# Column groups for the products of even and odd chunks at levels 32 and 64 of a gated recurrence

## The chip, the cores and the metric

One NeuronCore of a Trainium2 chip runs the whole kernel. The metric is device microseconds of one execution, as the median of several. Engines are named as in the profile: PE is TensorE's matrix multiplication, PEld its weight loads, DVE is VectorE, ACT is ScalarE, POOL is GpSimd, SP is SyncE.

## The reference, cut to what matters

A decoder layer on 1024 tokens of width 1024 in float32: a dilated attention and an HGRN2 recurrence, both fed by one large projection, merged by gates, then an output product and a norm. The change touches the recurrence alone. It has 8 heads with keys and values of 128:

```python
f = lb + (1.0 - lb) * jax.nn.sigmoid(f_raw)
k = 1.0 - f
# S_t = diag(f_t) S_{t-1} + k_t i_t^T;  o_t = S_t^T q_t
a = jnp.einsum('bhtk,bhsk,bhtsk->bhts', qc, kc, decay)
o_intra = jnp.einsum('bhts,bhsv->bhtv', a, vc)
```

The kernel takes chunks of 128 tokens, eight for each head, and needs for each chunk the 128 x 128 matrix `a` of decayed products of keys (rows, s) and queries (columns, t), for s up to t.

## The kernel before, in words

The kernel runs a projection (with products of split operands, three matmuls for each: lines 239 to 241), attention with more of the projection filled in between its steps, one branch product, the recurrence with the rest of the projection filled in, and the last two products. The change is in the recurrence stage, from about 553 to 960 us of the profiled span.

TensorE's instructions keep the order in which the program writes them (`manual_schedule` for PE); for the other engines the framework picks the order ahead of time. `recurrence(h)` is a generator: after each piece it yields an amount, and `fill(us)` then writes that many steps of the projection (`m` tiles, lines 239 to 241). The projection's weights are prepared two steps ahead: ACT casts them to `w_hi` (L246), DVE subtracts to `w_lo` (L224). A product's result is copied by ACT (L327) or added by DVE (L274).

In a head the chunk matrix is built by levels `hl` = 1, 2, 4, ..., 64. At a level the 1024 tokens fall into pairs of blocks of `hl`; the keys of the first block of a pair (`kk`) are multiplied with the decayed queries of the second (`qq`), and then DVE multiplies the decay of the level into `kk` (L1117) and `qq` (L1119) in place. Levels 1 to 16 go through `small()`: 32 matmuls with 32 stationary columns each, whose outputs go to the four groups of 32 partitions in turn (L1085). Their results are masked into `dg` by DVE (L1097, L1098) and copied into the diagonal blocks of `amat` (`am`) at L1135.

Level 32 has 16 matmuls in a burst (L1104), 32 stationary and 32 moving columns each. The first half of a chunk goes to partitions 0 to 31, the second to 64 to 95. Two ACT copies of 32 rows x 256 elements (L1107) bring them to `am`, rows in place. Level 64 has 8 matmuls (L1113), 64 stationary and 64 moving columns each, all of them to partitions 0 to 63, and one ACT copy of 64 x 512 (L1115). The stationary operand is a slice of `kk`, the moving one a slice of `qq`, all in float32, which the trace records as two loads and two matmuls for each matmul of the program. The results lie in `pp`, one bank of PSUM with two buffers.

After level 64 the keys are transposed (L1141), states are formed (L1153, L1157, L1159), and L1168 multiplies `am` with the values, L1170 the decayed queries with the states; the norm follows on ACT (L1173), DVE (L1175, L1177) and POOL (L1176), and its transposes (L1182) end the head.

Of the kernel before, what the change touches and what calls it, by code (L numbers as in the profile page):

```python
# [10 lines left out]
F32 = mybir.dt.float32  # L11
# [8 lines left out]
P = 128  # L20
# [159 lines left out]
def hybrid_layer(ctx: ExitStack, tc: tile.TileContext, x, w_ada, b_ada, w_in, w_branch_a, w_branch_b, w_out,  # L180
                 rel_bias, final_g, smalls, consts, onehot, logc, out, tap=None):
    nc = tc.nc
# [801 lines left out]
    with ExitStack() as ba:  # L984
# [5 lines left out]
        for m in range(4):  # L990
            for th in range(2):
                o, z = (b2p.tile([P, 512], F32, name="oar", bufs=7) for _ in range(2))
# [36 lines left out]
    with ExitStack() as hg:  # L1029
        g1 = hg.enter_context(tc.tile_pool(name="hg1", bufs=1, **right))  # L1030
        g2 = hg.enter_context(tc.tile_pool(name="hg2", bufs=2, **right))
        pp = hg.enter_context(tc.tile_pool(name="ps_p", bufs=2, **again))
# [5 lines left out]
        am = g1.tile([P, 8, P], F32, name="amat")  # L1038
        nc.gpsimd.memset(am, 0.0)
        qb = g1.tile([P, 2, S], F32, name="qb")  # L1040
        kk = g1.tile([P, S], F32, name="kk")
        qq = qb[:, 1]
        its, fqs, zss = {}, {}, {}

        def load_f(h):
            stream.need(f"f{h}")
            stream.need(f"h{h}")
            while turned.get(("i", h)) != 2:
                stream.step()
            fq = fqs[h] = g2.tile([P, S], F32, name="tot")  # L1050
            nc.sync.dma_start(fq, fb_d[h])
            nc.sync.dma_start(qb[:, 0], qb_d[h])
            it = its[h] = g2.tile([P, 8, P], F32, name="it")
            nc.sync.dma_start(it, ib_d[h])

        def load_z(h):
            zss[h] = []
            for th in range(2):
                z = g2.tile([P, 512], F32, name="zs")
                nc.sync.dma_start(z, zb_d[h][:, half_of(th)])  # L1060
                zss[h].append(z)
# [4 lines left out]
        def mask(n):  # L1066
            return kc[:, K_M + 32 * n:K_M + 32 * n + 32].unsqueeze(1).to_broadcast([P, 8, 32])

        def c3(t):
            return t.rearrange("p (c t) -> p c t", c=8)  # L1070

        def recurrence(h):
# [7 lines left out]
            def small(n):  # L1080
                pl = pp.tile([P, 512], F32, name="pp")[:, :256 * n].rearrange("p (c n t) -> p c n t", c=8, n=n)
                for c in range(8):
                    for b in range(4):
                        o = c * P + b * 32
                        nc.tensor.matmul(pl[32 * b:32 * b + 32, c], kk[:, o:o + 32], qb[:, 2 - n:2, o:o + 32],  # L1085
                                         start=True, stop=True)
                return pl

            n, hl = S // 2, 1
            while hl < P:  # L1090
                q4 = qq.rearrange("p (n two t) -> p n two t", two=2, t=hl)
                k4 = kk.rearrange("p (n two t) -> p n two t", two=2, t=hl)
                t3 = fq[:, :2 * n].rearrange("p (n two) -> p n two", two=2)
                if hl <= 16:
                    pl = small(2 if hl == 1 else 1)
                    if hl == 1:
                        nc.vector.tensor_tensor(d3, pl[:, :, 0], mask(0), ALU.mult)  # L1097
                    nc.vector.copy_predicated(d3, mask(1 + LEVELS.index(hl)).bitcast(I32), pl[:, :, 1 if hl == 1 else 0])  # L1098
                elif hl == 32:
                    pl = pp.tile([P, 512], F32, name="pp")[:, :256]  # L1100
                    for c in range(8):
                        for b in range(2):
                            o = c * P + 64 * b
                            nc.tensor.matmul(pl[64 * b:64 * b + 32, c * 32:c * 32 + 32], kk[:, o:o + 32],  # L1104
                                             qq[:, o + 32:o + 64], start=True, stop=True)
                    for b in range(2):
                        nc.scalar.copy(am[64 * b:64 * b + 32, :, 64 * b + 32:64 * b + 64],  # L1107
                                       c3(pl[64 * b:64 * b + 32]))
                else:
                    pl = pp.tile([P, 512], F32, name="pp")  # L1110
                    for c in range(8):
                        o = c * P
                        nc.tensor.matmul(pl[0:64, c * 64:c * 64 + 64], kk[:, o:o + 64], qq[:, o + 64:o + P],  # L1113
                                         start=True, stop=True)
                    nc.scalar.copy(am[0:64, :, 64:P], c3(pl[0:64]))  # L1115
                k_end = t3[:, :, 1:2].to_broadcast([P, n, hl])
                nc.vector.tensor_tensor(k4[:, :, 0, :], k4[:, :, 0, :], k_end, ALU.mult)  # L1117
                q_end = t3[:, :, 0:1].to_broadcast([P, n, hl])
                nc.vector.tensor_tensor(q4[:, :, 1, :], q4[:, :, 1, :], q_end, ALU.mult)  # L1119
                if fq is tot:  # L1120
                    tn = g1.tile([P, S // 2], F32, name="totn")
                    other = tot, tn
                else:
                    tn = other[0] if fq is other[1] else other[1]
                nc.vector.tensor_tensor(tn[:, :n], t3[:, :, 0], t3[:, :, 1], ALU.mult)
                fq = tn
                n //= 2
                hl *= 2
                yield 2.6
                if hl == 8:  # L1130
                    load_z(h)
                if hl == 32 and h + 1 < NHB:
                    load_f(h + 1)
# [14 lines left out]
            for g in range(2):  # L1148
                pu = pou.tile([P, 4, P], F32, name="pou")
                for cc in range(4):  # L1150
                    c = 4 * g + cc
                    if c < 7:
                        nc.tensor.matmul(pu[:, cc], kt[:, c], iv[:, c], start=True, stop=True)  # L1153
                for cc in range(4):
                    c = 4 * g + cc
# [7 lines left out]
            for g in range(2):  # L1163
                yield 1.9
                po = pou.tile([P, 4, P], F32, name="pou")
                for cc in range(4):
                    c = 4 * g + cc
# [30 lines left out]
        for h in range(NHB):  # L1198
            for us in recurrence(h):
                fill(us)  # L1200
# [250 lines left out]
```

## Time and profile before

| | |
|---|---|
| median of 3 runs | 1149.69 us (1147.69 to 1149.91) |
| the profiled execution's own time | 1151.74 us |
| its span, first to last instruction | 1149.9 us |
| mean granted clock of TensorE | 0.995 |
| PE busy | 97% of the span |
| DVE busy | 70% |
| ACT busy | 45% |

The span is the time between the first and the last instruction of the profiled execution; the rest of its own time lies around it. A busy share is the union of an engine's instructions. Matmuls are pipelined, so the duration of one is a latency, and what a burst of them costs is read from its first start to its last end. A line such as L1104 is a line of the kernel's file; a source line's matmul and its weight load are listed apart as PE and PEld.

### The profile page before, as it was taken

How to read it: one execution, taken by the hardware profiler on the slowest of the kernel's cores; microseconds unless marked ns; L12 is line 12 of the kernel's file. 1: busy time of each engine (PE TensorE's matmuls, PEld its weight loads, DVE VectorE, ACT ScalarE, POOL GpSimd, SP SyncE). 2: the span in 40 equal slices, each digit the busy share in tenths (PEclk: the TensorE clock that was granted, in tenths of full speed). 3: DMA queues.
4: the chain of work that ended last, by engine and by line, in shares of the span. 5: the costliest groups of instructions: out<-in, count | busy, mean ns of one | idle time of the engine just before them, and what ended most of it. 6: DMA issues, size and time to landing. Idle time of an engine off the chain costs nothing.

```text
span 1149.9 us, 21616 instructions
## 1 busy us (share of the span) xinstructions
PE 1113.1 (97%) x8266; PEld 908.7 (79%) x8266; DVE 809.0 (70%) x1607; ACT 517.8 (45%) x1059; POOL 117.7 (10%) x195
## 2 busy tenths in 40 slices
PE   5899999999999999999999999999999999999997
PEld 2677788888888888788877878787887878888886
DVE  3458888888877776753687787878888773769053
ACT  4565555578555555542234434343443432334021
POOL 1103032122202201100000000000000011000000
PEclk9999999999999999999999999999999999999999
DMA  9718576565556533746635253444435289864052
GB/s 311 225 37 248 175 209 179 152 165 145 139 139 154 153 100 104 269 158 215 223 103 171 78 185 100 160 140 137 158 101 176 81 259 325 290 213 133 29 183 75
DMA packets 161480, 189.54 MB, mean 165 GB/s; under 512 B 11312, under 2 KB 107696, under 8 KB 161376
## 3 DMA queue, kind: packets, MB, share of 16 engines
q1 hardware_dynamic: 140080, 153.95, 41.9%
q0 software_dynamic: 20896, 33.60, 11.7%
q8 instruction: 65, 1.06, 0.4%
q10 hardware_dynamic: 400, 0.61, 0.2%
q14 instruction: 39, 0.32, 0.1%
HBM read 129.36 MB, written 58.76 MB: 164 GB/s over the span
## 4 chain that ended last, share of the span: by engine, by line
PE 82%; DVE 7%; issue 6%; DMA 2%; ACT 2%; POOL 1%; ACTq 0%; POOLq 0%; DVEq 0%; SPq 0%
PE m L239 16%; PE m L241 15%; PE m L240 15%; PE pq L240 5%; PE pq L239 5%; PE pq L241 5%; PE pp L1085 3%; PE po L927 2%; PE pt L912 2%; PE pss L895 1%; PE pss L894 1%; PE pou L1168 1%; PE pou L1170 1%; PE pou L1153 1%; PE pmod L572 1%
## 5 line engine op out<-in xcount | busy, mean ns | idle before, releaser
L224 DVE TENSOR_TENSOR w_lo<-w_raw,w_hi 128x512 fp32r<-128x512 f32 x156 | 106.7, 686 | 49.6 <-ACT w_hi L246 45.8
L246 ACT CAST w_hi<-w_raw 128x512 fp32r<-128x512 f32 x146 | 90.4, 620 | 56.6 <-PE m L241 46.6
L327 ACT COPY ct<-m 128x512 f32<-128x512 f32 x90 | 52.6, 585 | 89.9 <-PE m L241 72.7
L246 ACT CAST w_hi<-w_s 128x512 fp32r<-128x512 f32 x90 | 55.8, 620 | 75.7 <-PE m L241 50.3
L274 DVE TENSOR_TENSOR ct<-m,ct 128x512 f32<-128x512 f32 x90 | 61.8, 687 | 27.7 <-PE m L241 26.1
L224 DVE TENSOR_TENSOR w_lo<-w_s,w_hi 128x512 fp32r<-128x512 f32 x90 | 61.9, 688 | 11.7 <-ACT w_hi L246 10.0
L900 ACT ACTIVATE s<-s,st 128x128 f32<-128x128 f32 (+3 forms) x64 | 49.8, 778 | 32.1 <-DVE st L897 32.1
L916 ACT CAST pth<-pt 128x512 fp32r<-128x512 f32 (+1 forms) x80 | 43.6, 544 | 36.3 <-PE pt L912 31.9
L224 DVE TENSOR_TENSOR ptl<-pt,pth 128x512 fp32r<-128x512 f32 (+1 forms) x80 | 50.5, 632 | 7.7 <-ACT pth L916 7.0
L239 PE MATMUL m<-b11h,w_hi 128*128 128x512 f32 x124 | 52.5, 424 | 2.0 <-DVE ct L274 2.0
L1176 POOL TENSOR_TENSOR ssh<-ssh,halfh 128x4 f32<-128x4 f32 x16 | 18.0, 1127 | 345.8 <-DVE ssh L1175 345.8
L239 PE MATMUL m<-b21h,w_hi 128*128 128x512 f32 x124 | 51.3, 414 | 0.6 <-ACT w_hi L246 0.6
L239 PE MATMUL m<-b22h,w_hi 128*128 128x512 f32 x124 | 50.9, 411 | 0.1
L239 PE MATMUL m<-t1h,w_hi 128*128 128x512 f32 x120 | 50.5, 421 | 0.0
L239 PE MATMUL m<-t2h,w_hi 128*128 128x512 f32 x120 | 49.6, 413 | 0.8 <-ACT ct L327 0.8
L239 PE MATMUL m<-t4h,w_hi 128*128 128x512 f32 x120 | 49.7, 414 | 0.4 <-DVE ct L274 0.4
L239 PE MATMUL m<-t3h,w_hi 128*128 128x512 f32 x120 | 49.7, 414 | 0.0
L241 PE MATMUL m<-b11l,w_hi 128*128 128x512 f32 x124 | 49.6, 400 | 0.0
L240 PE MATMUL m<-b11h,w_lo 128*128 128x512 f32 x124 | 49.2, 397 | 0.0
L240 PE MATMUL m<-b21h,w_lo 128*128 128x512 f32 x124 | 48.6, 392 | 0.2 <-DVE w_lo L224 0.2
L241 PE MATMUL m<-b21l,w_hi 128*128 128x512 f32 x124 | 48.8, 393 | 0.0
L241 PE MATMUL m<-b22l,w_hi 128*128 128x512 f32 x124 | 48.7, 393 | 0.0
(358 smaller groups left out, 3191.2 us busy)
## 6 DMA issues: line engine op xcount, KB each, us to landing
w_raw<-in_w_in_dram SPq DMA_DIRECT2D x128, 256.0 KB, 3.4
wa<-in_w_ada_dram SPq DMA_DIRECT2D x16, 512.0 KB, 8.7
qk_d<-ct SPq DMA_DIRECT2D x32, 256.0 KB, 3.4
k<-qk_d POOLq DMA_DIRECT2D x64, 128.0 KB, 4.9
qp<-qk_d POOLq DMA_DIRECT2D x32, 128.0 KB, 4.4
toep<-toep_d POOLq DMA_DIRECT2D x8, 512.0 KB, 6.2
vq_d<-ct SPq DMA_DIRECT2D x16, 256.0 KB, 2.6
vq<-vq_d POOLq DMA_DIRECT2D x16, 256.0 KB, 4.1
```

The costliest lines, as they stand in the source:

```text
L224: nc.vector.tensor_tensor(out_, a, hi.bitcast(F32), ALU.subtract)
L239: nc.tensor.matmul(ps, ah, bh, start=start, stop=False, skip_group_check=more)
L240: nc.tensor.matmul(ps, al, bh, start=False, stop=False, skip_group_check=more)
L241: nc.tensor.matmul(ps, ah, bl, start=False, stop=stop, skip_group_check=more)
L246: nc.scalar.copy(hi, src)
L274: nc.vector.tensor_tensor(out_, a, b_, op)
L327: nc.scalar.copy(c[name], b[which])
L900: nc.scalar.activation(s[:, :kw], s[:, :kw], AF.Exp, bias=prev, scale=-1.0, accum_out=st2[:, 2:3])
L912: nc.tensor.transpose(pt[:, c0:c0 + P], pn[b][:, kt * P:(kt + 1) * P], ident)
L916: nc.scalar.copy(pth[:, :w], pt[:, :w])
L927: nc.tensor.matmul(po[:, 256 - n:256], vq[kt // 4][:, kt % 4], src[:, c0:c0 + n], start=kt == 0 and a == 0, stop=kt == 2 * j + 1 and a == 1)
L1085: nc.tensor.matmul(pl[32 * b:32 * b + 32, c], kk[:, o:o + 32], qb[:, 2 - n:2, o:o + 32], start=True, stop=True)
```

## The change

At levels 32 and 64 the eight chunks of a head are told apart into even and odd ones. An even chunk's product is written to the partitions where it was, an odd one's to those `hl` further on, which at level 32 are the groups 32 to 63 and 96 to 127, and at level 64 the group 64 to 127. So the tile of results is half as wide: four chunks beside each other in place of eight. The matmuls are the same in number, shape and order. The copies to `am` are then made for even and odd chunks apart: four copies of 32 x 128 for two of 32 x 256, and two of 64 x 256 for one of 64 x 512. Those of the odd chunks read rows `hl` further on than they write.

```diff
-                elif hl == 32:
-                    pl = pp.tile([P, 512], F32, name="pp")[:, :256]
+                else:
+
+                    pl = pp.tile([P, 512], F32, name="pp")[:, :4 * hl].rearrange("p (c t) -> p c t", c=4)
                     for c in range(8):
-                        for b in range(2):
-                            o = c * P + 64 * b
-                            nc.tensor.matmul(pl[64 * b:64 * b + 32, c * 32:c * 32 + 32], kk[:, o:o + 32],
-                                             qq[:, o + 32:o + 64], start=True, stop=True)
-                    for b in range(2):
-                        nc.scalar.copy(am[64 * b:64 * b + 32, :, 64 * b + 32:64 * b + 64],
-                                       c3(pl[64 * b:64 * b + 32]))
-                else:
-                    pl = pp.tile([P, 512], F32, name="pp")
-                    for c in range(8):
-                        o = c * P
-                        nc.tensor.matmul(pl[0:64, c * 64:c * 64 + 64], kk[:, o:o + 64], qq[:, o + 64:o + P],
-                                         start=True, stop=True)
-                    nc.scalar.copy(am[0:64, :, 64:P], c3(pl[0:64]))
+                        for o in range(0, P, 2 * hl):
+                            to = o + hl * (c % 2)
+                            nc.tensor.matmul(pl[to:to + hl, c // 2], kk[:, c * P + o:c * P + o + hl],
+                                             qq[:, c * P + o + hl:c * P + o + 2 * hl], start=True, stop=True)
+                    pairs = am.rearrange("p (c two) t -> p two c t", two=2)
+                    for odd in range(2):
+                        for o in range(0, P, 2 * hl):
+                            nc.scalar.copy(pairs[o:o + hl, odd, :, o + hl:o + 2 * hl],
+                                           pl[o + hl * odd:o + hl * odd + hl])
```

## Rows read from the trace of the kernel before

**Rows 1.** The page: busy time by engine, and the granted clock by slices.

```profile
span 1149.9 us, 21616 instructions
...
PE 1113.1 (97%) x8266; PEld 908.7 (79%) x8266; DVE 809.0 (70%) x1607; ACT 517.8 (45%) x1059; POOL 117.7 (10%) x195
...
PEclk9999999999999999999999999999999999999999
```

**Rows 2.** The recurrence stage as one window: busy us of each engine.

```profile
core 0: us, PE busy (x) PEld busy (x) DVE busy (x) ACT busy (x) POOL busy (x), PEclk, DMA share, GB/s
553.00:960.00 407.00, 402.86 (x4720) 327.77 (x4719) 322.58 (x620) 162.39 (x378) 25.13 (x30) 1.00 0.48 153
```

**Rows 3.** The same window, first L1104's instructions alone, then L1113's.

```profile
553.00:960.00 407.00, 5.59 (x256) 4.73 (x256) 1.00 0.48 153
...
553.00:960.00 407.00, 9.16 (x128) 8.06 (x128) 1.00 0.48 153
```

**Rows 4.** Instructions on the tile pp: ns min/median/max, first and last start.

```profile
L1085 PE MATMUL pp<-qb,kk x2560: 189/196/243, 569.6 to 936.1; 128*32 128x32 f32 x158, 128*32 128x64 f32 x39
L1104 PEld LDWEIGHTS pp<-qb,kk x256: 106/113/113, 588.2 to 939.7; 128*32 128x32 f32 x128
L1104 PE MATMUL pp<-qb,kk x256: 189/196/217, 588.2 to 939.7; 128*32 128x32 f32 x128
L1113 PE MATMUL pp<-qb,kk x128: 222/222/270, 591.1 to 943.1; 128*64 128x64 f32 x128
L1107 ACT COPY amat<-pp x16: 346/364/367, 589.0 to 940.7; 32x256 f32<-32x256 f32 x16
L1115 ACT COPY amat<-pp x8: 576/583/583, 592.3 to 943.3; 64x512 f32<-64x512 f32 x8
```

**Rows 5.** Timeline, first head: start, length and records of each burst.

```profile
569.64 1.10 PE L1085 MATMUL pp<-qb,kk 128*32 128x64 f32 x64
...
584.58 0.76 PE L1085 MATMUL pp<-qb,kk 128*32 128x32 f32 x64
...
588.23 0.59 PEld L1104 LDWEIGHTS pp<-qb,kk 128*32 128x32 f32 x32 [0.35 <-issue]
588.23 0.70 PE L1104 MATMUL pp<-qb,kk 128*32 128x32 f32 x32
...
591.12 1.15 PE L1113 MATMUL pp<-qb,kk 128*64 128x64 f32 x16
```

**Rows 6.** ACT's groups by shape, whole span: copies of 256 elements.

```profile
L932 ACT COPY t<-po 64x256 f32<-64x256 f32 x32 | 11.8, 370 | 19.1 <-PE po L927 18.9
...
L574 ACT COPY row<-pmod 128x256 f32<-128x256 f32 x8 | 3.0, 373 | 16.9 <-PE pmod L572 16.9
```

**Rows 7.** Waits in the recurrence stage: us in total, times, longest.

```profile
DVE w_lo L224 <- ACT w_hi L246: 18.4, 20, 2.2
...
ACT amat L1115 <- PE pp L1113: 8.3, 7, 2.2
...
ACT amat L1107 <- PE pp L1104: 5.8, 5, 2.9
...
DVE kk L1117 <- PE pp L1113: 2.5, 2, 1.4
```

**Rows 8.** Chain that ended last, a stretch with DVE in it.

```profile
787.44 0.24 PE m L241
787.68 0.02 issue
787.70 0.69 DVE ct L274
788.39 0.01 issue
788.40 0.69 DVE w_lo L224
789.09 0.36 DVE dg L1098
...
790.49 0.61 DVE qb L1119
791.10 0.14 issue
791.23 0.70 PE pp L1104 x31
```

## The prediction

> **What bounds the kernel now.** I read the page first. PE is busy for 97% of the span and its clock was granted in full in every slice, so no part of this change can be won or lost by the clock [rows 1]. A share over the span says little about one stage, so next I took the recurrence stage as one window: PE 402.86 of 407.00 us, DVE 322.58, ACT 162.39 [rows 2]. PE therefore stands still for 407.00 - 402.86 = 4.1 us in the whole stage. The other engines have their order and their waits, but PE sets the pace: what a burst of matmuls takes there is time on the path, unless something that PE needs comes late.
>
> Then the same window for the two changed lines: L1104 takes 5.59 us and L1113 9.16 us, in eight bursts each, one for each head [rows 3]. So 14.75 us is all that the change can touch on PE; even deleting the matmuls would give no more than 1.3% of the time. What it adds lies on ACT, so I looked at what ACT makes others wait for [rows 7], and, in the chain that ended last, at what happens where PE isn't the last to arrive [rows 8].
>
> **Level 32: four groups of columns in place of two.** A burst is 32 records in 0.699 us (5.59 / 8). A record has a latency of 0.196 [rows 4], so the starts are (0.699 - 0.196) / 31 = 16.2 ns apart. The trace holds the same matmul on four groups: L1085 at the levels 2 to 16 has the same 128x32 operands, with outputs to the four groups in turn, and there 64 records take 0.76 us [rows 5]: (0.76 - 0.196) / 63 = 9.0 ns. Twice the groups, nearly half the spacing, so the spacing is a queue for each group, not one for the array. After the change L1104 is L1085 with half the records: 0.196 + 31 x 9.0 = 0.47 us. It saves 0.23 us a head. Bounds: nothing (spacing stays at 16.2), and 0.25 (two groups to four at exactly half, 8.1).
>
> **Level 64: two groups in place of one.** A burst is 16 records in 9.16 / 8 = 1.145 us, latency 0.222 [rows 4], so (1.145 - 0.222) / 15 = 61.5 ns apart. No row shows 64 stationary columns on two groups, so this one is bounded. From above: spacing unchanged, nothing saved. From below: the first level's burst has the same 64 moving columns on four groups of 32, 64 records in 1.10 us [rows 5], taking 0.22 for the latency (1.10 - 0.22) / 63 = 14.0 ns, which is 56 ns for each group; on two groups that is 28 ns, and the burst 0.222 + 15 x 28 = 0.64 us, 0.50 saved. I take half of the measured 61.5, 30.8 ns: 0.222 + 15 x 30.8 = 0.68 us, 0.46 saved. I choose near the lower end because one group at 64 moving columns (61.5) and one of four (56) are spaced alike, as they should be if each group has its own queue.
>
> [...] In L1104 before, 32 loads of 0.113 us each fit into 0.59 us, beside 32 matmuls in 0.70 [rows 4, 5], so they do overlap, and I go by the rows.
>
> Sum on PE: 0.23 + 0.46 = 0.69 us a head, 8 heads: 5.5 us; bounds 0 and 8 x (0.25 + 0.50) = 6.0. The number of bursts is unchanged, so what it costs to come into and out of one is left out.
>
> **The copies on ACT.** Before: two of 32x256 at 0.364 and one of 64x512 at 0.583 [rows 4], 1.31 us a head. The two new copies of level 64 have 64 x 256 elements; L932 is just that, and it too reads rows 64 to 127 and writes 0 to 63: 0.370 [rows 6]. A copy of 128 partitions without a move takes 0.373 [rows 6], so moving rows costs nothing. Level 64: 2 x 0.37 = 0.74, 0.16 more. The 32 x 128 copies have no row. From 256 and 512 elements, 0.364 and 0.583, each element costs 0.86 ns and the rest is 0.145 us, so 128 give an estimate of 0.255: four are 1.02, 0.29 more. Bounds: 0.182 (half of 256 elements; no more than before) and 0.364 (all overhead; 0.73 more). ACT gets 0.45 us a head, 3.6 in all; bounds 0.16 and 0.89 a head.
>
> I cost this at nothing on the path. The cover is that ACT waits at just these places: 8.3 us in seven waits at L1115 and 5.8 in five at L1107, for the matmuls to end [rows 7]. These now end earlier. Level 64's copies end 0.46 - 0.16 = 0.30 us earlier than before, level 32's 0.29 - 0.23 = 0.06 later. Queued behind them on ACT is the cast `w_hi` (L246), then `w_lo` on DVE, then a product; they are made two steps ahead. `amat` itself is read at L1168, after the transposes and the states. Without that cover 0.45 us a head would count, 3.6 us. DVE gains a little: L1117 overwrites `kk` when the level's matmuls have read it, and it waited 2.5 us for L1113 [rows 7]. Three copies more on ACT's queue are the only added instructions; no DMA, no queue of SP or POOL is moved.
>
> **What comes through.** Where PE waits, it is for chains like this: product, DVE L274, L224, L1098, L1117, L1119, then L1104 [rows 8]. They start from a matmul, so they shift as a whole. But an engine in order with a backlog of its own doesn't shift fully, and DVE is busy for 79% of the stage (322.58 / 407) [rows 2]. I take off a tenth: 5.5 - 0.5 = 5.0 us. The profiled execution took 1151.74 us with a span of 1149.9; its own span should fall to about 1144.9. The median of the runs is 2.05 below that execution's time, and the same 5.0 off it give 1149.69 - 5.0 = 1144.7.
>
> **The rivals.**
>
> *Only level 32 gains.* If 64 stationary columns take the array's loading path for both groups, 61.5 ns stay. For it: no row shows two groups of 64. Against: the two kinds of one-group spacing above. The time: 8 x 0.23 = 1.8 saved, 1147.9. A DVE that absorbs two thirds of the sum gives about the same.
>
> *The change doesn't do what it says.* Spacing unchanged at both levels, or all of it eaten by waits for DVE: 1149.7. For it: 4.1 us idle on PE, which could grow to about 9 without any engine being full. Against: four groups against two [rows 5]. [...]
>
> *Slower: ACT's copies hold back the casts.* If a 32 x 128 copy costs as much as one of 256 elements, ACT has 0.89 us a head more. Where `w_hi` stands right behind it and DVE waits for it, as it did 20 times for 18.4 us [rows 7], the product waits too. It decides once more than 0.69 / 0.89 = 78% of it reaches PE; at all of it, 8 x (0.89 - 0.69) = 1.6 us slower, and with the saving of level 32 alone 8 x (0.89 - 0.23) = 5.3 slower: 1151 to 1155. Against: ACT is busy for 162 of 407 us [rows 2]. [...]
>
> **How the numbers follow.** The sum, with between 70% and all of it coming through: 0.74. Only level 32, or most absorbed: 0.13. No change: 0.08. Slower: 0.05. About 0.2%, 2.3 us, is what a measurement of this kernel can tell from no change. Faster by more takes the first case and a quarter of the second: 0.77. Slower by over 0.2% is most of the last, and some of the spread of the runs themselves (1147.69 to 1149.91): 0.05. Within it: 0.18. The likeliest time is 1144.7. Range: from 6.0 saved with 0.9 for the spread of runs, 1142.8, to the edge of the second case, 1148.3; that leaves the last two cases and some of the second outside.
>
> **What would show it.** In the profile after: the bursts of level 32 at 0.47 us and of level 64 at 0.68, 3.8 and 5.5 us in all; ACT copies of 128 elements near 0.255 and of 256 at 0.37; PE's idle time in the stage not over some 4.7 us; the stage, and with it the span, 5 us shorter, with nothing moved before 580 us. It would be wrong if the level 64 burst stays over 1 us (the queue isn't each group's), if PE's idle grows by several us (DVE takes it back), or if waits of DVE for `w_hi` grow behind the new copies.

## The result, and the profile after

The changed kernel took 1142.66 us (median of 4 runs, 1141.85 to 1143.38) against 1148.83 for the kernel before, a ratio of 0.9946 with a 95% interval of 0.9929 to 0.9963: 6.2 us less. A second series gave 1143.76 against 1149.24, a ratio of 0.9956 (0.9945 to 0.9968), by that ratio 5.1 us less. The forecast was 1144.7 us and 5.0 less, with a range from 1142.8: the first median lies 0.14 us below it, the second inside. Both levels' products are now on L1105, all of ACT's copies to `amat` from these levels on L1110.

The page of the changed kernel, span and busy time by engine:

```profile
span 1141.6 us, 21637 instructions
PE 1105.4 (97%) x8266; PEld 901.9 (79%) x8266; DVE 808.7 (71%) x1607; ACT 521.4 (46%) x1083; POOL 117.0 (10%) x195
```

Against [rows 1] PE is busy for 7.7 us less with the same number of instructions; ACT has 24 instructions and 3.6 us more. Of PE's 7.7 us, 5.5 lie in the recurrence stage. The stage as one window, its edges moved with the work, and then L1105 alone:

```profile
550.20:951.60 401.40, 397.37 (x4720) 322.20 (x4719) 322.14 (x620) 165.93 (x402) 24.73 (x30) 1.00 0.48 155
...
550.00:953.00 403.00, 9.15 (x384) 7.18 (x384) 1.00 0.48 156
```

PE stands still for 401.40 - 397.37 = 4.0 us, as it did before (4.1, [rows 2]). The two lines of [rows 3] had 14.75 us between them; 9.15 are left, so 5.60 are gone. The timeline, first the start of the first head, then its two bursts with ACT's copies, then the last burst of the last head:

```profile
566.87 1.10 PE L1085 MATMUL pp<-qb,kk 128*32 128x64 f32 x64
...
585.48 0.46 PE L1105 MATMUL pp<-qb,kk 128*32 128x32 f32 x32
586.07 1.06 ACT L1110 COPY amat<-pp 32x128 f32<-32x128 f32 x4
588.14 0.69 PE L1105 MATMUL pp<-qb,kk 128*64 128x64 f32 x16
588.93 0.74 ACT L1110 COPY amat<-pp 64x256 f32<-64x256 f32 x2
...
934.22 0.69 PE L1105 MATMUL pp<-qb,kk 128*64 128x64 f32 x16
```

The bursts went from 0.70 and 1.15 us [rows 5] to 0.46 and 0.69; four copies of 32 x 128 take 1.06 us, two of 64 x 256 0.74. From the first start to the last end it is 934.22 + 0.69 - 566.87 = 368.04 us. The same stretch of the kernel before runs from 569.64 [rows 5] to the end of this burst:

```profile
942.13 1.15 PE L1113 MATMUL pp<-qb,kk 128*64 128x64 f32 x16
```

942.13 + 1.15 - 569.64 = 373.64 us. So the stretch lost 5.60 us, as much as its bursts: in this pair of profiles all of it came through. The second profile of either kernel (its run is below) has 373.56 and 367.95 us for the same stretch, 5.61 less. The first two profiles differ by 8.3 us in span (1149.9 to 1141.6); 2.77 of that were there at the first start (569.64 to 566.87), before any changed instruction. Waits in the changed kernel's stage (us in total, times, longest):

```profile
DVE w_lo L224 <- ACT w_hi L246: 18.0, 20, 2.2
...
ACT amat L1110 <- PE pp L1105: 10.2, 10, 2.7
```

ACT still waits for the products at its copies, 10.2 us where it was 8.3 + 5.8, and DVE waits for the casts about as long as before (18.0 us, 18.4 in [rows 7]).

### The profile page after: what moved, and what is told of

Its sections match the earlier page's. It is cut to its first block, busy times and chain, and to the rows that moved or that the text cites. A ratio compares the mean times of both kernels' runs of the same rounds, so it can differ in the third digit from the quotient of the medians.

```text
span 1141.6 us, 21637 instructions
## 1 busy us (share of the span) xinstructions
PE 1105.4 (97%) x8266; PEld 901.9 (79%) x8266; DVE 808.7 (71%) x1607; ACT 521.4 (46%) x1083; POOL 117.0 (10%) x195
## 3 DMA queue, kind: packets, MB, share of 16 engines
q8 instruction: 65, 1.06, 0.4%
## 4 chain that ended last, share of the span: by engine, by line
PE 81%; DVE 6%; issue 6%; DMA 3%; ACT 2%; POOL 1%; SPq 0%; POOLq 0%; ACTq 0%; DVEq 0%
PE m L239 16%; PE m L241 15%; PE m L240 15%; PE pq L240 5%; PE pq L239 5%; PE pq L241 5%; PE pp L1085 3%; PE po L927 2%; PE pt L912 2%; PE pss L895 1%; PE pss L894 1%; PE pou L1164 1%; PE pou L1166 1%; PE pou L1149 1%; PE pmod L572 1%
## 5 line engine op out<-in xcount | busy, mean ns | idle before, releaser
L274 DVE TENSOR_TENSOR ct<-m,ct 128x512 f32<-128x512 f32 x90 | 61.7, 686 | 26.1 <-PE m L241 24.5
```

The lines of the kernel that those rows point to most:

```text
L274: nc.vector.tensor_tensor(out_, a, b_, op)
```

## The experiments

Theory: each group of columns takes its own records one after another, groups run side by side, and PE's gain reaches the end in full while ACT's longer copies cost nothing. Rivals: DVE takes back a part; the copies cost something; the 2.8 us ahead of the stage belong to the change.

**Both kernels once more.** No edit.

> The changed kernel once more, in five rounds. If the change is worth what its sixteen bursts lost (8 x (0.24 + 0.46) = 5.6 us, all of it reaching the end), the median lies 5.6 us under that of the kernel before, a ratio of 0.9951. If DVE took back a tenth, as the prediction had it, 5.0 us and 0.9956. If the 2.8 us that the changed kernel's profile was ahead when the first changed matmul began belong to the change, 8.4 us and 0.993.

> The kernel before against itself. Chance theory: the 2.8 us come and go between executions of one and the same program, 2.1 of them in the branch A stage around 475 to 488 us, where the clock granted to TensorE was 0.91 in the first profile of before and 1.00 in that of the changed kernel; then this profile starts its first burst of level 32 somewhere between 585.4 and 588.3 us, the times spread over some 2 us, and the ratio is 1.000. Rival: they are the change's (other addresses of tiles or code); then this profile agrees with the first one of before within 0.3 us, with the clock down again.

Measured: the changed kernel 0.9956 (0.9945 to 0.9968); the kernel before against itself 1.0008 (0.9996 to 1.002), with single runs of it from 1146.09 to 1151.45 us. 5.6 us would be 0.9951, inside both intervals of the changed kernel; 5.0 (0.9956) is inside them too, so the totals can't tell a tenth. 8.4 us (0.993) is outside the second. In its new profile the kernel before starts its first head at 568.64 us, 1.0 earlier than in its first profile, and the change can't have done that. A difference between the two lies in the branch A stage. Windows there (busy us of PE, PEld, DVE, ACT and POOL, then the granted clock, the share of time in which DMA engines were busy and GB/s); the first profile of before:

```profile
484.00:488.00 4.00, 2.78 (x9) 2.22 (x10) 3.69 (x7) 3.91 (x8) 0.00 (x0) 0.82 0.56 183
488.00:492.00 4.00, 4.00 (x15) 3.21 (x14) 3.96 (x8) 3.34 (x8) 0.00 (x0) 0.75 0.60 194
```

Its second profile, the same program:

```profile
484.00:488.00 4.00, 2.76 (x12) 2.18 (x12) 3.62 (x7) 3.83 (x8) 0.00 (x0) 1.00 0.68 240
488.00:492.00 4.00, 3.65 (x16) 2.91 (x16) 3.96 (x8) 3.39 (x7) 0.00 (x0) 1.00 0.59 189
```

In the first, PE stood still for 2.0 us in one piece, waiting for DVE's L274, took up work again at 485.2, and from 486.6 to 490.0 the granted clock was 0.50; as means of these windows that is 0.82 and 0.75. Matmuls of the projection started 0.43 us apart there, in place of 0.23. In the second profile it stood still as long but in two pieces, the longer 1.6, and the clock stayed at 1.00. PE had 9 + 15 matmuls under way in these windows in the first, 12 + 16 in the second. Eight other profiles, the second of before and seven of kernels with the change or a part of it, have 1.00 as the mean of 470 to 495 us, where the first of before has 0.93.

How much of the 2.77 us is chance these profiles alone can't tell: the first head starts at 568.6 and 569.6 us in the two of before, and between 564.3 and 567.8 in all ten of kernels with the change or a part of it. Two totals further down can. The runs with the even chunks first and with the products twice have the changed kernel's tiles and copies, but their bursts lost 2.2 us and gained 0.56 us against the kernel before. If the change gave 2.77 us besides, they would come out at 0.9957 and 0.9981; measured are 0.9985 (0.9974 to 0.9996) and 1.0003 (0.9991 to 1.0015). So the rival falls: by the first of them, at most some 0.8 us ahead of the stage can be the change's.

**Each level alone.** The new branch for one level, the old code for the other:

```diff
-                else:
+                elif hl == 32:
...
+                else:
+                    pl = pp.tile([P, 512], F32, name="pp")
+                    for c in range(8):
+                        o = c * P
+                        nc.tensor.matmul(pl[0:64, c * 64:c * 64 + 64], kk[:, o:o + 64], qq[:, o + 64:o + P],
+                                         start=True, stop=True)
+                    nc.scalar.copy(am[0:64, :, 64:P], c3(pl[0:64]))
```

The other run keeps `elif hl == 32` with the old code and has the new branch as its `else`.

> Level 32 as changed, level 64 as before. A queue for each group and everything passed on: burst of level 32 at 0.46 us, of level 64 at 1.145, and 8 x 0.24 = 1.9 us faster (ratio 0.9983). If DVE takes back a tenth or more: 1.7 or less. If the extra ACT time of level 32 (4 x 0.25 for 2 x 0.36, so 0.3 us a head) came through, 8 x 0.3 = 2.4 us would be lost again and nothing would be left.

> Level 64 as changed, level 32 as before. A queue for each group and everything passed on: bursts of 0.699 and 0.686 us, 8 x 0.46 = 3.7 us faster (ratio 0.9968). The two levels add up: this and the run with level 32 alone sum to the whole change. If a level's gain is taken back by the wait for DVE that comes next, each alone gives more than its share, and they sum to more than the whole.

Measured: level 32 alone 0.998 (0.9967 to 0.9993), level 64 alone 0.9966 (0.9955 to 0.9977), which is 2.3 and 3.9 us less. Their bursts took 0.46 and 1.15 us, and 0.70 and 0.69. The sum, 6.2, agrees with the whole change within the intervals, which are too wide to exclude that a little is taken back. In their profiles the stretch takes 371.77 and 369.87 us, 1.8 and 3.7 less than the mean of the two profiles of before, and these add up to the whole change's 5.6. The prediction's rival in which only level 32 gains falls. Extra copies that eat level 32's gain are not there either: its interval leaves out 1.000.

**Even chunks first, then odd ones.**

```diff
-                    for c in range(8):
+                    for c in (0, 2, 4, 6, 1, 3, 5, 7):
```

> The changed kernel with its products in another order: chunks 0, 2, 4, 6, then 1, 3, 5, 7. Matmuls, groups and copies are the same, but neighbours no longer alternate between an even and an odd chunk's group. A queue for each group, matmuls taken in order: spacing back at 61.5 ns at level 64 but for the one change of group in the middle, and at 16.2 ns at level 32; bursts of about 1.10 and 0.69 us; as slow as the kernel before, while ACT still has the six copies. Then the time is also the price of the copies by themselves: 1.000 if they are hidden, up to 8 x 0.45 = 3.6 us slower (1.003) if not. Rival, that TensorE takes matmuls out of order or that only the number of groups counts: bursts at 0.46 and 0.69 as in the changed kernel.

Measured: 0.9985 (0.9974 to 0.9996), 1.7 us less than before. The timeline of the first head:

```profile
586.36 0.60 PE L1105 MATMUL pp<-qb,kk 128*32 128x32 f32 x32
...
589.16 0.97 PE L1105 MATMUL pp<-qb,kk 128*64 128x64 f32 x16
```

It met neither expectation. The groups and their number are those of the changed kernel, and some 60% of the gain is gone: over the stage L1105 takes 12.57 us, between 9.15 and 14.75. So the order counts, not the number of groups. But the bursts are shorter than the expectation's estimates for an order kept strictly (0.69 and 1.10). The trace's start times of single records show why, in the burst of level 64 above. One row of eight records, most of them 58 ns apart, runs from 0 to 457 ns after the burst's start; a second row of eight, spaced alike, starts at 288 and ends its starts at 744. A part of the burst:

```profile
L1105 PE MATMUL pp<-qb,kk x9: 222/222/270, 589.3 to 589.6; 128*64 128x64 f32 x9
```

The first record of a row lasts 270 ns, the others 222, and here, behind the burst's own first, is one of 270. The trace doesn't name the chunks, but the even ones stand first in the program, so the second row is the odd ones': TensorE started them while three records of the even ones were still to start. TensorE's instructions are written in the program's order, and started a little out of it. Of the copies it says little: 14.75 - 12.57 = 2.2 us of bursts saved, 1.7 measured, with an interval from 0.5 to 3.0.

**Runs of two.**

```diff
-                    for c in range(8):
+                    for c in (0, 2, 1, 3, 4, 6, 5, 7):
```

> The changed kernel with the chunks in the order 0, 2, 1, 3, 4, 6, 5, 7: two products to one group, then two to the other. With all even chunks first, a burst of level 64 took 0.966 us, between the 1.145 of one group and the 0.686 of strict alternation, and the odd chunks' first record started while four of the even ones' were still to come. If TensorE can start a record past some four older ones that wait for another group, runs of two products (four records) are within reach: bursts near 0.69 at level 64 and 0.46 to 0.5 at level 32, and the changed kernel's time (ratio 0.995). If records start in the program's order but for chance, each change of group costs a wait: about 0.85 at level 64, some 1.5 us slower than the changed kernel in all.

Measured: 0.9956 (0.994 to 0.9973). The bursts take 0.48 us at level 32 and 0.73 at level 64:

```profile
585.54 0.73 PE L1105 MATMUL pp<-qb,kk 128*64 128x64 f32 x16
```

Two products (four records) to one group before the other's turn cost 0.02 and 0.04 us a burst. The bursts are where the first reading of the expectation had them, 0.73 us at level 64 and not the second's 0.85, and strict alternation wasn't needed here.

**Quarters at level 64.**

```diff
+                            for s in range(0, hl, 32):
-                            nc.tensor.matmul(pl[to:to + hl, c // 2], kk[:, c * P + o:c * P + o + hl],
-                                             qq[:, c * P + o + hl:c * P + o + 2 * hl], start=True, stop=True)
+                                nc.tensor.matmul(pl[to + s:to + s + 32, c // 2],
+                                                 kk[:, c * P + o + s:c * P + o + s + 32],
+                                                 qq[:, c * P + o + hl:c * P + o + 2 * hl], start=True, stop=True)
```

> The changed kernel with each product of level 64 made as two of 32 stationary columns and 64 moving ones, so that it goes to all four groups: 32 records in place of 16. It tells what spaces the records of a group. If it is the 64 moving columns (56 ns for a group in the first level's burst), 32 records at 14 ns: 0.22 + 31 x 0.014 = 0.65 us, 0.03 us a head less than now and no difference in time. If it is the stationary columns (a group of 32 at level 32 is spaced by 32 ns), 32 records at 8 ns: 0.22 + 31 x 0.008 = 0.47 us and 8 x 0.22 = 1.7 us faster than the changed kernel.

Measured: 0.9957 (0.9938 to 0.9975), no other than the changed kernel.

```profile
586.00 0.65 PE L1106 MATMUL pp<-qb,kk 128*32 128x64 f32 x32
```

Twice the records in 0.65 us: (0.65 - 0.22) / 31 = 13.9 ns, 55 for each of the four groups of 32 stationary columns, where the rows of 64 above had 58. So a group's spacing went by the 64 moving columns here, and hardly by the stationary ones. Four groups gave next to nothing more at level 64: 0.65 us a burst for 0.69. In this one profile the stretch is 369.46 us, 1.4 more than the changed kernel's though the bursts are shorter; PE stood still once for 2.3 us before a burst of L1085, for which the profile names no cause.

**The products twice.**

```diff
-                    for c in range(8):
+                    for c in 2 * list(range(8)):
```

> The changed kernel with the products of levels 32 and 64 each made twice, the second on top of the first: 32 more records at 8 ns and 16 more at 31 ns, 0.25 and 0.49 us a head. Everything on PE is passed on: 8 x 0.74 = 5.9 us slower than the changed kernel, which is the time of the kernel before (ratio 1.000). If DVE's chains hid a tenth or more of what PE gains, then they also hide it where PE loses: 5.3 us or less (0.9995 or under).

Measured: 1.0003 (0.9991 to 1.0015). The first head starts at 567.11 us; the last two bursts:

```profile
936.85 0.76 PE L1105 MATMUL pp<-qb,kk 128*32 128x32 f32 x64
939.83 1.15 PE L1105 MATMUL pp<-qb,kk 128*64 128x64 f32 x32
```

The bursts are 0.30 and 0.46 longer than the changed kernel's; over the stage L1105 takes 15.31 us in place of 9.15, 6.16 more. The stretch takes 939.83 + 1.15 - 567.11 = 373.87 us, 5.83 more than 368.04. Added work comes through to 95% in this profile. The ratio itself lies 6.0 us above the 0.9951 that the bursts of the changed kernel would give, and can't tell 95 from 100%.

**The copies twice, and six times.**

```diff
-                        for o in range(0, P, 2 * hl):
+                        for o in 2 * list(range(0, P, 2 * hl)):
                             nc.scalar.copy(pairs
```

> The changed kernel with each of the six copies to amat made twice: 8 x 1.8 = 14 us more on ACT. If the copies are hidden because ACT has room and the casts are made two steps ahead: the changed kernel's time within 0.1%, ratio to the kernel before 0.995. If the prediction's slower rival has its mechanism (casts held back behind the copies), a part of the 14 us shows: some 8 x 1.8 x 0.5 = 7 us at a half, and DVE's waits for w_hi grow from 18 us.

Measured: 0.9942 (0.993 to 0.9954). 14 us more on ACT cost nothing that an interval of 1.4 us to either side can show; that the 3.6 us which the changed kernel has more than the kernel before cost nothing either follows from it. The same with 6 in place of 2:

> The changed kernel with each copy to amat made six times: 8 x 5 x 1.75 = 70 us more on ACT, in blocks of 6 us at level 32 and 4.4 us at level 64 in which no cast can start. Made twice, the copies cost nothing. If the cover is the casts' two steps of lead, some 5.5 us, it is used up here: each head loses what the blocks have over the cover, 1 to 5 us, so 8 to 40 us in all (ratio to the kernel before 1.002 to 1.03), and PE waits for w_lo. If ACT's room in the stage alone counts (about 230 us idle of 403), still nothing: ratio 0.995.

Measured: 1.0159 (1.0139 to 1.018), 0.021 over the changed kernel: some 24 us of the 70. The size is as expected from a cover that is used up, the place is another. The two longest waits of PE in the stage (us in total, times, longest):

```profile
PE pou L1149 <- ACT kt L1138: 9.8, 13, 1.6
PE pou L1164 <- DVE st L1155: 4.8, 5, 1.9
```

No wait of PE for `w_lo` is in the whole answer. The transposed keys (`kt`) are copied on ACT behind and among the copies to `amat`, and the states' products wait for them. So the cover of the copies ends first at the recurrence's own next step. The casts aren't cleared by this: DVE's waits for `w_hi` grew from 18.0 to 38.6 us, and PE waits 4.8 us for the states (`st`), which DVE makes in the same queue. How much of the 24 us came that way isn't settled. A part may be the clock's: it was 0.99 as the mean of 550 to 970 us, where the changed kernel has 1.00 from 550 to 953; a hundredth of the 398.78 us that PE was busy there, some 4 us, is an estimate of what this cost.

## Why the prediction was right and wrong

**Level 32, 0.23 us a head: right.** It measured 0.70 - 0.46 = 0.24. Taking the level's spacing from L1085, the same shape on four groups, was the right reading.

**Level 64, 0.46 us a head: right.** 1.145 - 0.69 = 0.46. No row had shown two groups of 64; half the spacing of one group was the right choice between the bounds, and the traces show why: at 64 moving columns a group had nearly the same spacing whether it was 32 or 64 wide (56 ns between its records in the first level's burst, 58 in the bursts of L1113). The weight loads overlapped with the matmuls after the change too: in the changed kernel's first burst of level 32, 32 loads of 0.113 us each lie in 0.35 us, beside 32 matmuls in 0.46, and alternating the column groups took the bursts from 14.75 to 9.15 us over the stage.

**The copies at nothing: right.** 0.255 was the estimate for 128 elements; four took 1.06 us, 0.26 each. The copies that move rows took 0.37 as foreseen. Made twice they still cost nothing. The slower rival's general idea, copies that hold back what is queued behind them on ACT, does exist, but only with far more copies, and there it is seen first at `kt`; whether the casts it named have a part in it stays open.

**What comes through: this step was mis-sized.** The prediction took a tenth off, 5.5 to 5.0, for a DVE that is busy for 79% of the stage and has a backlog of its own. The tenth was its author's estimate, and no run shows it. In both pairs of profiles nothing was taken off: bursts 5.60 us less, stretch 5.60 and 5.61 us less, PE's idle time 4.0 against 4.1. That fits the prediction's own earlier sentence, that the chains in which PE waits for DVE start from a matmul and shift as a whole; the busy share of DVE was no reason to take anything off. This is some 0.6 us of the 2.0 between 1144.7 and 1142.66. It isn't what put the time outside the range, whose lower end allowed for 6.0.

**The range: this margin was mis-sized too.** It went down from 1149.69 by 6.0 and by 0.9 for the spread of runs. 1149.69 was the median of three runs that lay 2.2 us apart. With a fourth it became 1148.83: the base moved by 0.86 us and used up nearly all of the 0.9. The later medians of the kernel before were 1149.24, 1148.77 and 1149.25 us, and single runs of it lay up to 3.8 us under the first. 1148.83 - 5.6 = 1143.2 would have been in the range; the last 0.6 us to 1142.66 are within the spread of runs, and no run gives them another cause. That the first series fell 0.14 us outside and the second, 1143.76, inside is chance, as far as these runs tell.

**The clock: misread, without harm to the sum.** The prediction took the page's line for a clock "granted in full in every slice", but its digit 9 stands for 90% or more, and a fall to 0.50 for 3.4 us doesn't show in a slice of 29. The one in the branch A stage of the first profile is no work of the change. It is part of why two profiles can't be compared by their spans, but it didn't move the prediction's base, which was the median of the other runs.

## What to carry to other kernels

Where a stationary operand has 32 or 64 columns, as here, let neighbouring matmuls write to different groups of output partitions: that took a float32 burst on one group of 64 from 1.15 to 0.69 us, and one on two groups of 32 from 0.70 to 0.46. It is the order that does it; runs of two did nearly as well, and four even chunks before four odd ones lost some 60% of it. Where PE sets the pace and its own idle time is 1% of the stage, as here, count a shorter burst in full. Read the gain inside the stretch that the change touches, where two profiles of one kernel agreed to 0.1 us, and give the range the spread of single runs, which was 5 to 7 us here, when its base is the median of three.

## What had not been expected of the hardware

TensorE started records of one group ahead of older ones of the other: with four even chunks before four odd ones the odd ones' first record started 288 ns into a level-64 burst, the even ones' last at 457 ns, and the burst took 0.97 us, where an order kept strictly would have given 1.10 by the expectation's estimate. A group's spacing went by the moving columns and hardly by the stationary ones (32 stationary columns in quarters, 64 in halves: 0.65 and 0.69 us for the same products).
